# Weight blocks split whole instead of in halves, in a two-layer decoder trunk in split fp32

## The chip, the cores and the metric

The kernel runs on one core of one Trainium2 chip. The metric is the device time of one execution in microseconds (us), the median of several runs.

## The reference

A token matrix `x` (256 tokens, 2048 wide) goes through two layers, each a token mixer followed by a SwiGLU. A vector `c` gives a shift, a scale and a gate for every sub-layer.

```python
for i in range(2):
    sh1, sc1, g1, sh2, sc2, g2 = split(silu(c) @ w_mod[i] + b_mod[i], 6)
    h = rms_norm(x, norm1_g[i]) * (1 + sc1) + sh1
    y = retention_mixer(h, ...) if i == 0 else short_conv_mixer(h, ...)   # 8 heads / width 3
    x = x + g1 * y
    h = rms_norm(x, norm2_g[i]) * (1 + sc2) + sh2
    a, b = split(h @ ffn_w_in[i], 2)                  # 2048 -> 2 x 5632
    x = x + g2 * ((silu(a) * b) @ ffn_w_out[i])       # 5632 -> 2048
return rms_norm(x, final_g)
```

All of it is in float32, and all weights are read once.

## The kernel before

**Split products.** TensorE multiplies in a type with a shorter mantissa (`float32r`). Every float32 operand is therefore split in two: `hi`, the operand cast to the short type, and `lo`, what is left (`lo = raw - hi`). A product is then three matmuls: hi by hi, hi by lo, lo by hi. The tokens' side is split when it is made. The weights are split as they stream in.

**The weight stream.** All layer weights lie in `w_all` as 456 blocks of 128 partitions by 2048 columns (1 MB each), in the order of use. `fetch` (L370) starts the load of the next block into one of three buffers `raw`. `prepare` (L376) takes the next *piece* of a block: ScalarE casts it (`nc.scalar.copy(hi, raw)`, L402), then VectorE subtracts (`lo = raw - hi`, L405). In the kernel before a piece is half a block, 1024 columns; `hi` and `lo` have four buffers of 1024 columns each (`PART_BUFS`). `take` (L410) hands the matmuls their columns. Each time a piece is used up, `take` calls `prepare` until the piece in use and two more are ready (`AHEAD`; three more in the last stage, `ahead_now`). A cast has to wait until the matmuls on the buffer's old content are done. VectorE and ScalarE each work through their queue in order; the order was set by a scheduler when the program was built, except in the opening, where it is the order of the code. TensorE's order is the order of the code throughout.

**The modulation.** `modulation` (L313) needs one 1 MB block of `w_mod` for each 128 entries of a shift, scale or gate: the load takes one of the same three `raw` buffers, and VectorE multiplies and sums it in one instruction (L318). 32 of them stand in the opening (L755), 160 are spread over the kernel by `paced`.

**The stages.** The opening computes the first norm and the first weights' products beside the modulation, with both engines' order written by hand. Then come the retention's heads and its output product, the SwiGLU of layer 0, the short convolution, and the SwiGLU of layer 1, the *last stage*.

**The last stage and its sevens.** Here the roles are turned round: 128 tokens by 128 rows are the weights of the array, and 512 columns of a weight block are streamed. `gathered` (L1269) goes through the *rows* of one pass: a row is one block, two row tiles by two column tiles of 512. A plain row is 24 matmuls (`by_token`). Three rows of each pass are *sevens* (`Seven`, L155): a Strassen-Winograd product of 2 by 2 parts, seven products (`thrice`) of three matmuls each instead of eight. For that the block's four parts B11, B12, B22, B21 (the four 512 columns of `b`) are turned into

- T1 = B12 - B11 and T3 = B22 - B12, written to `differences` (L391, one VectorE instruction, a buffer that there is once),
- T2 = B22 - T1, written over B12 (L395),
- T4 = B21 - T2, written over B21 after B21 has been split (L397).

Before, the pieces of a seven are four: (B22, B21), (T1, T3), (B11, T2), T4. `uses` (L158) gives the order of the products.

A pass of `last_input` (ten of them) has eight rows, of which rows 3, 4 and 6 are sevens (`IN_SEVEN`), so that 3 and 4 follow each other. Before row 2 of the next pass, `turned` brings the result back to the other layout: eight transposes on TensorE (L1331), copies on ScalarE, two subtractions on VectorE (L1336). In five of the ten passes it also makes the sums of tokens that later sevens need (`tokens_sums_of`, L1143 to L1146, and a `split`). In three passes it does not, and in two passes there is no `turned`: the results of the last pass of each part are turned inside the following `last_output`. `mixed_sums` (L1243 to L1246) and four sums (L1317) close a pass. A pass of `last_output` (four of them) has sevens at positions 2, 4 and 6, so that a plain row follows each seven.

Of the kernel before, what the change touches and what calls it, by code (L numbers as in the profile page):

```python
# [11 lines left out]
F32R = mybir.dt.float32r  # L12
I32 = mybir.dt.int32
AF = mybir.ActivationFunctionType
ALU = mybir.AluOpType
PSUM = bass.MemoryType.PSUM

P = 128
# [7 lines left out]
DV = 512  # L26
# [5 lines left out]
CHUNK = 2048  # L32
HALF = 1024
# [11 lines left out]
AHEAD = 2  # L45
# [2 lines left out]
MOD_PRIO = -300  # L48
STEPS = (8, 8, 20)
RAW_BUFS = 3  # L50
PART_BUFS = 4
LEFT, ENDS, EARLIER = 8, 2, 120

Q0, K0, V0, G0 = 0, HEADS * DK, 2 * HEADS * DK, 2 * HEADS * DK + HEADS * DV
# [3 lines left out]
class Group:  # L58
# [11 lines left out]
    def uses(self):  # L70
        return [(self, k, c, w) for k in self.ks for c, w in self.items]
# [70 lines left out]
class Seven:  # L142
# [6 lines left out]
    n = 2 * DV // P  # L149
# [6 lines left out]
        return [(i, a, DV), (i, b, DV), (j, b, DV), (j, a, DV)]  # L156

    def uses(self):  # L158
        return [(self, None, n, DV) for n in ("B22", "B21", "T1", "T3", "B11", "T2", "T4")]


def in_pairs(cols, rows, sevens):
# [94 lines left out]
def trunk(ctx: ExitStack, tc: tile.TileContext, x_in, c_in, pos_in, w_mod, cols_in, gain_in, tab_in, w_all, out):  # L257
    nc = tc.nc
    const = ctx.enter_context(tc.tile_pool(name="const", bufs=1))
    work = ctx.enter_context(tc.tile_pool(name="work", bufs=2))  # L260
    wpool = ctx.enter_context(tc.tile_pool(name="wpool", bufs=PART_BUFS))
    ps = ctx.enter_context(tc.tile_pool(name="ps", bufs=8, space=PSUM))
# [3 lines left out]
    def name(s):  # L266
        serial[0] += 1
        return f"{s}_{serial[0]}"

    def tmp(tag, shape=(P, S), dtype=F32, pool=work, bufs=None):  # L270
        return pool.tile(list(shape), dtype, tag=tag, name=name(tag), bufs=bufs)
# [9 lines left out]
    x = [t[:, j, :] for t in x4 for j in range(4)]  # L281
    n_cols = cols_in.shape[1]
    cols = const.tile([P, n_cols], F32, tag="cols", name="cols")
    at = [0]
# [16 lines left out]
    differences = flat[2]  # L301
# [35 lines left out]
    early = sum(g.n * len(g.ks) for g in RET_SPANS)  # L337
# [15 lines left out]
    def needed(layer, which, last=KT - 1):  # L353
        while any(m[:2] == (layer, which) and m[2] <= last for m in todo):
            modulation(*todo.pop())
# [6 lines left out]
    in_seven, n = set(), 0  # L362
# [2 lines left out]
            in_seven.add(n // CHUNK)  # L365
        n += g.n * P * len(g.ks)

    pieces = [(i, p) for i in range(w_all.shape[0]) for p in ((2, 3, 4, 5) if i in in_seven else (0, 1))]

    def fetch():  # L370
        raw = wpool.tile([P, CHUNK], F32, tag="raw", name=name("raw"), bufs=RAW_BUFS)
# [4 lines left out]
    def prepare(between=None):  # L376
        if prepared[0] == len(pieces):
            return
        _, piece = pieces[prepared[0]]
        prepared[0] += 1  # L380
        if piece in (0, 2):
            if not fetched:
                fetch()
            raws[:] = [fetched.pop(0)]
            while first <= units[0] < early and len(fetched) < RAW_BUFS - 1 and n_fetched[0] < w_all.shape[0]:
                fetch()
        whole = raws[0]
        b = [whole[:, i : i + DV] for i in range(0, CHUNK, DV)]
        raw = whole[:, :HALF] if piece in (0, 4) else whole[:, HALF:]
        if piece == 2:  # L390
            nc.vector.tensor_tensor(differences, whole[:, DV : 3 * DV], whole[:, : 2 * DV], op=ALU.subtract)  # L391
        elif piece == 3:
            raw = differences
        elif piece == 4:
            nc.vector.tensor_tensor(b[1], b[2], differences[:, :DV], op=ALU.subtract)  # L395
        elif piece == 5:
            nc.vector.tensor_tensor(b[3], b[3], b[1], op=ALU.subtract)  # L397
            raw = b[3]
        width = raw.shape[1]
        hi = wpool.tile([P, HALF], F32R, tag="hi", name=name("hi"))[:, :width]  # L400
        lo = wpool.tile([P, HALF], F32R, tag="lo", name=name("lo"))[:, :width]
        nc.scalar.copy(hi, raw)  # L402
        if between:
            between()
        nc.vector.tensor_tensor(lo, raw, hi.bitcast(F32), op=ALU.subtract)  # L405
        ready.append((hi, lo, width))

    prepared, ahead_now = [0], [AHEAD]

    def take(group, k, col, width=P):  # L410
# [89 lines left out]
        return banks  # L500

    def summed(pt, dst=None, at=slice(0, S)):
        low = tmp("low", bufs=3)
        nc.scalar.copy(low[:, at], pt[:, 1, at])
        dst = tmp("sum", bufs=4) if dst is None else dst
        nc.vector.tensor_tensor(dst, pt[:, 0, at], low[:, at], op=ALU.add)
        return dst
# [96 lines left out]
    def normed(accs, layer, norm, g):  # L604

        needed(layer, SH2 if norm else SH1)  # L610
        shift = mod_s[layer][norm].unsqueeze(2)
        ends = [raw_all[:, :, i : i + 1] for i in range(ENDS)]
        nc.scalar.copy(ends[0], shift)
        nc.vector.tensor_tensor(ends[1], shift, ends[0].bitcast(F32), op=ALU.subtract)
        banks = [bank().rearrange("p a b -> p (a b)")[:, : S + 2] for _ in g.cols]
        made = [0]

        def more(n):
            while made[0] < n:
                modulated(h[made[0]], made[0], root, layer, norm)  # L620
                made[0] += 1

        for k in g.ks:
            high, low = raw_all[:, k, : ENDS + S], raw_all[:, k, ENDS + S :]
            for c, pt in zip(g.cols, banks):
                hi, lo = take(g, k, c)
                nc.tensor.matmul(pt, hi, high, start=k == 0, stop=False, skip_group_check=True)  # L627
                nc.tensor.matmul(pt[:, 2:], hi, low, start=False, stop=False, skip_group_check=True)  # L628
                nc.tensor.matmul(pt, lo, high, start=False, stop=k == KT - 1, skip_group_check=True)  # L629
            if k == ROOTS_AT:  # L630
                r = norm_roots(norm_sums(accs), D)
            elif k == SPREAD_AT:
                root = tmp("rb", bufs=1)
                nc.scalar.copy(root, norm_spread(r))
            elif k > SPREAD_AT:
                more(min(k, made[0] + 2))
        more(KT)
        paced(len(g.cols) * len(g.ks))

        def total(pt, dst=None):  # L640
            low_end = tmp("end", (P, 1), bufs=4)
            nc.scalar.copy(low_end, pt[:, 1:2])
            end = tmp("end", (P, 1), bufs=4)
            nc.scalar.activation(end, pt[:, 0:1], AF.Identity, bias=low_end)
            t = tmp("low", bufs=3)
            nc.vector.tensor_tensor(t, pt[:, 2:], root, op=ALU.mult)
            dst = tmp("sum", bufs=4) if dst is None else dst
            nc.scalar.activation(dst, t, AF.Identity, bias=end)
            return dst

        return [lambda dst=None, pt=pt: total(pt, dst) for pt in banks]
# [27 lines left out]
    with ExitStack() as inner:  # L679
# [64 lines left out]
        with tc.tile_pool(name="start", bufs=1) as sp:  # L744
# [133 lines left out]
            at = 0.0  # L878
# [205 lines left out]
    for i, g in enumerate(CONV_IN):  # L1084
        pending += [sums(g)] if i else normed(acc, 1, 0, g)
        while len(pending) >= 3:
# [3 lines left out]
            b, c, u = pb(tmp("bsum", pool=mpool, bufs=2)), pc(), pu()  # L1090
# [67 lines left out]
    def made_in_sums():  # L1158

        tmp("beside_sums", (P, BESIDE_SUMS), bufs=1)  # L1160
        for tag, n in (("u", 3), ("low", 3), ("sum", 4)):
            single_sums.extend(tmp(tag, (P, 2, P), F32R, bufs=n) for _ in range(n))
        for i in IN_SEVEN:
            both = tmp("u512", (P, 2, S), pool=mpool, bufs=3)
            for n in range(2):
                k = 2 * i + n
                high, low = [h[k].bitcast(F32)[:, v, :] for v in range(2)]
                nc.vector.tensor_tensor(both[:, n, :], high, low, op=ALU.add)
            in_sums[i] = [single_sums.pop() for _ in range(3)]
            tokens_sums_of(*parts(both), h[2 * i][:, :, P:], in_sums[i])  # L1170
# [53 lines left out]
    def sevens(g, act, base, sums, ours, banks, first, last):  # L1224

        s1, s2, s4 = [[v[:, n, :] for n in range(2)] for v in sums]
        (a11, s3), (a12, a22) = [[half_of(act[k - base], t) for t in range(2)] for k in g.ks]
        p1, p5, p6, p7 = [(b, first, last) for b in banks]
        for use, x, (o, a, z) in zip(g.uses(), (s4, a12, s1, s3, a11, s2, a22), (
            (ours[0, 1], False, False), (ours[0, 0], False, False), p5, p7, p1, p6, (ours[1, 0], False, False)  # L1230
        )):
            thrice(o, x, take(*use), a, z)
            if use[2] in ("B21", "T3", "T2"):
                paced(4)
        paced(4)

# [151 lines left out]
    for part in range(2):  # L1388
        n = LAST_TILES[part] // 2
        mid = mids(LAST_TILES[part]) if part else first_mid  # L1390
        if not part:
            first_rows(mid[-2:])
            made_in_sums()
            ahead_now[0] = AHEAD + 1
        for i, groups in enumerate(LAST_IN[part]):
            due = OUT_SEVEN[part]
            seven = [tokens_sums[due.index(q)] if q in due else None for q in (2 * i, 2 * i + 1)]
            last_input(groups, mid[2 * i : 2 * i + 2], seven)
        act = [mid[k // 2][:, k % 2] for k in range(2 * n)]
        for c, groups in enumerate(LAST_OUT[part]):  # L1400
            last_output(part, 2 * c, groups, act, part * LAST_TILES[0])
# [37 lines left out]
```

## Time and profile before

| | us |
|---|---|
| median of 3 runs | 2593.82 |
| lowest and highest run | 2591.88, 2595.02 |
| span of the profiled execution | 2591.5 |
| TensorE busy | 2563.3 |
| VectorE busy | 2197.4 |
| ScalarE busy | 1306.0 |

The span runs from the first to the last instruction of one profiled execution; no device time of that execution itself is given, and the runs lie 0.4 to 3.5 us above its span. The profile names engines PE (TensorE), PEld (its weight load), DVE (VectorE), ACT (ScalarE), POOL (GpSimd) and SP (the queue of the loads). A group of instructions is shown as line, engine, operation, output<-input, shape and count, then busy time, mean ns of one, and the idle time of the engine just before them with what ended it.

### The profile page before, as it was taken

To read this page: it belongs to the slowest core of one execution; us is meant where nothing else is said; L and a number is where in the kernel's file an instruction comes from. 1 tells how busy PE (TensorE), PEld (TensorE's weight loads), DVE (VectorE), ACT (ScalarE), POOL (GpSimd) and SP (SyncE) were. 2 spreads that over 40 slices of the span, in tenths; PEclk is the share of its full clock that TensorE was granted. 3 is DMA by queue.
4 is the path that set the end of the run, shared out by engine and by line. 5 is a ranking of instruction groups with operands and counts; after the bars stand their busy time and mean duration, and the time that the engine had idled before them with its cause. 6 is when DMAs were issued, how large, how long until landed. Compare 5 with 4: busy or idle time off the path is not lost.

```text
span 2591.5 us, 36408 instructions
## 1 busy us (share of the span) xinstructions
PE 2563.3 (99%) x14181; PEld 2236.3 (86%) x14181; DVE 2197.4 (85%) x2762; ACT 1306.0 (50%) x1792; POOL 125.9 (5%) x232
## 2 busy tenths in 40 slices
PE   7999999999999999999999999999999999999998
PEld 6898889888889888888888898888998888888887
DVE  7988978787698887777778889988989998999978
ACT  5544543444456545334444454444565554556554
POOL 0000000110000000100001001000000000000001
PEclk9999999999999999999999999999999999999999
DMA  9975768767676888777877768877845565555654
GB/s 398 388 293 209 268 243 306 300 248 277 251 282 246 330 323 307 301 296 298 298 294 283 298 237 313 330 297 277 308 165 210 188 223 205 180 210 187 222 208 147
DMA packets 96688, 689.56 MB, mean 266 GB/s; under 512 B 10737, under 2 KB 12161, under 8 KB 13441
## 3 DMA queue, kind: packets, MB, share of 16 engines
q1 hardware_dynamic: 96514, 687.23, 71.3%
q8 instruction: 111, 1.82, 0.3%
q14 instruction: 63, 0.52, 0.1%
HBM read 685.08 MB, written 2.11 MB: 265 GB/s over the span
## 4 chain that ended last, share of the span: by engine, by line
PE 94%; DVE 3%; DMA 2%; issue 1%; ACT 1%; ACTq 0%; POOLq 0%; POOL 0%; DVEq 0%
PE bank L447 30%; PE bank L450 16%; PE bank L461 12%; PE bank L460 12%; PE bank L462 12%; PE bank L495 2%; PE bank L496 2%; PE bank L494 2%; PE bank L627 1%; PE bank L629 1%; PE bank L628 1%; DVE raw L755 1%; DMA raw<-w_all 1%; DVE lo L405 1%; PE bank L983 1%
## 5 line engine op out<-in xcount | busy, mean ns | idle before, releaser
L402 ACT CAST hi<-raw 128x1024 fp32r<-128x1024 f32 (+1 forms) x954 | 978.9, 1033 | 1015.8 <-PE bank L447 346.4
L405 DVE TENSOR_TENSOR lo<-raw,hi 128x1024 fp32r<-128x1024 f32 (+1 forms) x954 | 1133.9, 1197 | 322.6 <-ACT hi L402 317.3
L447 PE MATMUL bank<-h,hi 128*128 128x512 f32 x2016 | 699.3, 390 | 0.0
L450 PE MATMUL bank<-h,lo 128*128 128x256 f32 x2016 | 568.5, 282 | 0.0
L447 PEld LDWEIGHTS bank<-h,hi 128*128 128x128 f32 x2016 | 378.4, 188 | 79.2
L460 PE MATMUL bank<-hi,h 128*128 128x512 f32 x1032 | 405.0, 392 | 2.2 <-DVE rm L739 2.2
L461 PE MATMUL bank<-lo,h 128*128 128x512 f32 x1032 | 404.3, 392 | 0.0
L462 PE MATMUL bank<-hi,h 128*128 128x512 f32 x1032 | 402.7, 390 | 0.0
L450 PEld LDWEIGHTS bank<-h,lo 128*128 128x128 f32 x2016 | 381.0, 189 | 0.1
L318 DVE SCALAR_TENSOR_TENSOR raw<-raw,cb 128x2048 f32<-128x2048 f32 x160 | 365.5, 2284 | 15.7 <-DMA raw<-w_mod 15.3
L447 PE MATMUL bank<-mid,hi 128*128 128x512 f32 x922 | 319.8, 390 | 0.0
L450 PE MATMUL bank<-mid,lo 128*128 128x256 f32 x922 | 260.1, 282 | 0.4 <-DVE lo L405 0.4
L460 PEld LDWEIGHTS bank<-hi,h 128*128 128x128 f32 x1032 | 194.4, 188 | 40.7 <-DVE rm L739 2.8
L462 PEld LDWEIGHTS bank<-hi,h 128*128 128x128 f32 x1032 | 194.2, 188 | 40.8
L461 PEld LDWEIGHTS bank<-lo,h 128*128 128x128 f32 x1032 | 194.5, 188 | 40.4 <-DVE lo L405 3.3
L447 PEld LDWEIGHTS bank<-mid,hi 128*128 128x128 f32 x922 | 173.1, 188 | 36.2
L450 PEld LDWEIGHTS bank<-mid,lo 128*128 128x128 f32 x922 | 174.2, 189 | 0.7 <-DVE lo L405 0.7
L447 PE MATMUL bank<-rm,hi 128*128 128x512 f32 x496 | 172.5, 390 | 0.0
L496 PE MATMUL bank<-h,lo 128*128 128x256 f32 x512 | 146.4, 286 | 4.6 <-DVE lo L405 4.6
L494 PE MATMUL bank<-h,hi 128*128 128x256 f32 x512 | 146.1, 285 | 3.4 <-ACT h L783 3.4
L495 PE MATMUL bank<-h,hi 128*128 128x256 f32 x512 | 146.1, 285 | 0.7 <-DVE h L784 0.7
L450 PE MATMUL bank<-rm,lo 128*128 128x256 f32 x496 | 139.8, 282 | 0.0
(256 smaller groups left out, 3197.4 us busy)
## 6 DMA issues: line engine op xcount, KB each, us to landing
raw<-w_all SPq DMA_DIRECT2D x456, 1024.0 KB, 4.8
raw<-w_mod SPq DMA_DIRECT2D x192, 1024.0 KB, 5.2
x<-x_in SPq DMA_DIRECT2D x4, 512.0 KB, 5.3
out<-xt SPq DMA_DIRECT2D x4, 512.0 KB, 3.0
decay<-tab_in SPq DMA_DIRECT2D x8, 128.0 KB, 2.4
x<-gate_row SPq DMA_DIRECT2D x2, 512.0 KB, 4.8
last_gain<-gain_in SPq DMA_DIRECT2D x1, 1024.0 KB, 7.2
cols<-cols_in SPq DMA_DIRECT2D x1, 152.0 KB, 8.3
```

The source lines that it names most:

```text
L318: nc.vector.scalar_tensor_tensor(raw, raw, 1.0, cb, op0=ALU.mult, op1=ALU.mult, accum_out=total)
L402: nc.scalar.copy(hi, raw)
L405: nc.vector.tensor_tensor(lo, raw, hi.bitcast(F32), op=ALU.subtract)
L447: nc.tensor.matmul(pt, hi, h, start=fresh and k == g.ks[0], stop=False, skip_group_check=True)
L450: nc.tensor.matmul(pt[:, 1, :], lo, h[:, 0, :], start=False, stop=last and k == g.ks[-1], skip_group_check=True)
L460: nc.tensor.matmul(o, hi, w_hi, start=first, stop=False)
L461: nc.tensor.matmul(o, hi, w_lo, start=False, stop=False)
L462: nc.tensor.matmul(o, lo, w_hi, start=False, stop=last)
L494: nc.tensor.matmul(pt, hi, h[:, 0, :], start=first, stop=False, skip_group_check=True)
L495: nc.tensor.matmul(pt, hi, h[:, 1, :], start=False, stop=False, skip_group_check=True)
L496: nc.tensor.matmul(pt, lo, h[:, 0, :], start=False, stop=last, skip_group_check=True)
L627: nc.tensor.matmul(pt, hi, high, start=k == 0, stop=False, skip_group_check=True)
```

## The change

Behind the opening a plain block is one piece: one cast and one subtraction of 2048 columns (piece 5). The blocks of the opening stay in halves (pieces 0 and 1), but both halves go into one buffer. `hi` and `lo` have three buffers of 2048 columns instead of four of 1024. A seven has three pieces: the whole block with T2 already in the place of B12 (piece 2), the differences (piece 3), and T4 (piece 4); the last two share a buffer. The order of a seven's products is changed to fit: B11, T2, B22, B21, T1, T3, T4. `ahead_now` stays at two pieces in the last stage. The room for the larger buffers comes from one buffer `low` less and from the reserved space of the descriptor ring, which goes from its default to 512.

```diff
-PART_BUFS = 4
+PART_BUFS = 3
...
-        return [(self, None, n, DV) for n in ("B22", "B21", "T1", "T3", "B11", "T2", "T4")]
+        return [(self, None, n, DV) for n in ("B11", "T2", "B22", "B21", "T1", "T3", "T4")]
...
-    pieces = [(i, p) for i in range(w_all.shape[0]) for p in ((2, 3, 4, 5) if i in in_seven else (0, 1))]
+    halved = early * P // CHUNK
+    pieces = [
+        (i, p) for i in range(w_all.shape[0])
+        for p in ((2, 3, 4) if i in in_seven else (0, 1) if i < halved else (5,))
+    ]
...
-        if piece in (0, 2):
+        if piece in (0, 2, 5):
...
-        raw = whole[:, :HALF] if piece in (0, 4) else whole[:, HALF:]
-        if piece == 2:
+        raw, at = whole, 0
+        if piece in (0, 1):
+            raw = whole[:, piece * HALF : (piece + 1) * HALF]
+            at = piece * HALF
+        elif piece == 2:
             nc.vector.tensor_tensor(differences, whole[:, DV : 3 * DV], whole[:, : 2 * DV], op=ALU.subtract)
+            nc.vector.tensor_tensor(b[1], b[2], differences[:, :DV], op=ALU.subtract)
         elif piece == 3:
             raw = differences
         elif piece == 4:
-            nc.vector.tensor_tensor(b[1], b[2], differences[:, :DV], op=ALU.subtract)
-        elif piece == 5:
             nc.vector.tensor_tensor(b[3], b[3], b[1], op=ALU.subtract)
-            raw = b[3]
+            raw, at = b[3], HALF
         width = raw.shape[1]
-        hi = wpool.tile([P, HALF], F32R, tag="hi", name=name("hi"))[:, :width]
-        lo = wpool.tile([P, HALF], F32R, tag="lo", name=name("lo"))[:, :width]
+        if at == 0:
+            both[:] = [wpool.tile([P, CHUNK], F32R, tag=tag, name=name(tag)) for tag in ("hi", "lo")]
+        hi, lo = [t[:, at : at + width] for t in both]
         nc.scalar.copy(hi, raw)
...
-        low = tmp("low", bufs=3)
+        low = tmp("low", bufs=2)
...
-        for use, x, (o, a, z) in zip(g.uses(), (s4, a12, s1, s3, a11, s2, a22), (
-            (ours[0, 1], False, False), (ours[0, 0], False, False), p5, p7, p1, p6, (ours[1, 0], False, False)
+        for use, x, (o, a, z) in zip(g.uses(), (a11, s2, s4, a12, s1, s3, a22), (
+            p1, p6, (ours[0, 1], False, False), (ours[0, 0], False, False), p5, p7, (ours[1, 0], False, False)
...
-            if use[2] in ("B21", "T3", "T2"):
+            if use[2] in ("T2", "B21", "T3"):
...
-            ahead_now[0] = AHEAD + 1
...
-    nc = bacc.Bacc("TRN2", target_bir_lowering=False, num_devices=1)
+    nc = bacc.Bacc("TRN2", target_bir_lowering=False, num_devices=1, dynamic_dma_scratch_size=512)
```

More of the change, by code (lines that the diff above doesn't have):

```diff
@@ L406, in prepare @@
         ready.append((hi, lo, width))
+    both = []
     prepared, ahead_now = [0], [AHEAD]
@@ L644, in total @@
             nc.scalar.activation(end, pt[:, 0:1], AF.Identity, bias=low_end)
-            t = tmp("low", bufs=3)
+            t = tmp("low", bufs=2)
             nc.vector.tensor_tensor(t, pt[:, 2:], root, op=ALU.mult)
@@ L1160, in made_in_sums @@
         tmp("beside_sums", (P, BESIDE_SUMS), bufs=1)
-        for tag, n in (("u", 3), ("low", 3), ("sum", 4)):
+        for tag, n in (("u", 3), ("low", 2), ("sum", 4)):
             single_sums.extend(tmp(tag, (P, 2, P), F32R, bufs=n) for _ in range(n))
```

## The prediction

> **What bounds the kernel now.** I read the page's shares first, then the stages, then one pass of the last stage.
>
> ```profile
> span 2591.5 us, 36408 instructions
> ...
> PE 2563.3 (99%) x14181; PEld 2236.3 (86%) x14181; DVE 2197.4 (85%) x2762; ACT 1306.0 (50%) x1792; POOL 125.9 (5%) x232
> ...
> PE 94%; DVE 3%; DMA 2%; issue 1%; ACT 1%; ACTq 0%; POOLq 0%; POOL 0%; DVEq 0%
> ```
>
> TensorE is busy 99% of the span and holds 94% of the chain that ended last. What it does not use is 28 us. The table by stage (us, then busy us of PE, PEld, DVE, ACT) tells where that is:
>
> ```profile
> 0.00:128.00 128.00, 110.67 (x625) 93.37 (x625) 110.56 (x121) 71.97 (x112) 1.57 (x5) 1.00 0.98 397
> 128.00:810.00 682.00, 681.03 (x3951) 603.45 (x3952) 561.61 (x722) 321.64 (x444) 42.78 (x74) 1.00 0.71 266
> 810.00:1530.00 720.00, 720.00 (x4234) 641.47 (x4233) 578.38 (x695) 342.00 (x489) 53.70 (x104) 1.00 0.80 299
> 1530.00:1890.00 360.00, 359.57 (x2190) 323.40 (x2189) 320.52 (x457) 175.16 (x257) 19.84 (x41) 1.00 0.79 292
> ...
> 1935.00:2105.00 170.00, 170.00 (x762) 139.87 (x762) 157.36 (x185) 98.23 (x114) 0.00 (x0) 1.00 0.58 204
> 2105.00:2210.00 105.00, 104.46 (x463) 86.23 (x462) 90.20 (x105) 54.03 (x59) 0.00 (x0) 1.00 0.56 202
> 2210.00:2460.00 250.00, 250.00 (x1118) 205.81 (x1117) 231.69 (x274) 145.06 (x167) 0.00 (x0) 1.00 0.56 201
> ```
>
> 17.3 us of it lie in the opening. From 128 to 2460 us TensorE is idle for 1.9 us in all. So the body has nothing to win, and the question is where this change makes TensorE wait. In the last stage (from 1935 us) VectorE is 93% busy: 157.36 of 170, 231.69 of 250. There it has no room.
>
> **One pass of the last stage now.** Between two turns of the result (eight transposes, from the chain) lies one pass of eight rows:
>
> ```profile
> 2019.30 0.87 PE bank L1331 x8
> ...
> 2061.91 0.87 PE bank L1331 x8
> ```
>
> That is 42.61 us. Its matmuls follow at this distance:
>
> ```profile
> 2000.10 0.39 PE L460 MATMUL bank<-hi,h 128*128 128x512 f32 x1
> 2000.32 0.39 PE L461 MATMUL bank<-lo,h 128*128 128x512 f32 x1
> 2000.55 0.39 PE L462 MATMUL bank<-hi,h 128*128 128x512 f32 x1
> 2000.78 0.39 PE L460 MATMUL bank<-hi,h 128*128 128x512 f32 x1
> ```
>
> 0.68 us for three, 0.227 each. A plain row (24) takes 5.44 us, a seven (21) 4.76; five, three and the turn make 42.35. TensorE loses 0.25 us in a pass. VectorE in the same pass:
>
> ```profile
> L405 DVE TENSOR_TENSOR lo<-raw,hi 128x1024 fp32r<-128x1024 f32 x16 | 19.4, 1220 | 2.4 <-ACT hi L402 2.2
> L405 DVE TENSOR_TENSOR lo<-x,hi 128x1024 fp32r<-128x1024 f32 x3 | 3.7, 1221 | 0.2 <-ACT hi L402 0.2
> ```
>
> It idles 2.6 us of 42.6, for casts. Any new idle time beyond that and it is VectorE that sets the pass.
>
> **What the wider instructions cost.** ScalarE first, then VectorE, over the whole span:
>
> ```profile
> L402 ACT CAST hi<-raw 128x1024 fp32r<-128x1024 f32 x912 | 953.9, 1052 | 980.2 <-PE bank L447 346.4 <-PE bank L462 305.6 <-DMA raw<-w_all 179.9
> ...
> L402 ACT CAST hi<-raw 128x512 fp32r<-128x512 f32 x42 | 26.1, 620 | 35.6 <-PE bank L462 32.3 <-DVE lo L405 3.3
> ```
>
> ```profile
> L405 DVE TENSOR_TENSOR lo<-raw,hi 128x1024 fp32r<-128x1024 f32 x912 | 1107.2, 1221 | 315.9 <-ACT hi L402 310.8
> ...
> L405 DVE TENSOR_TENSOR lo<-raw,hi 128x512 fp32r<-128x512 f32 x42 | 28.8, 686 | 6.7 <-ACT hi L402 6.5
> ```
>
> From 512 to 1024 columns the cast grows by 432 ns and the subtraction by 535. Twice that on top gives 1.92 us for a whole cast and 2.29 for a whole subtraction, estimates by a straight line. Two halves take 2.10 and 2.44: each whole block saves 0.18 us on ScalarE and 0.15 on VectorE. In a queue without waits the distance of two subtractions is shorter than their length, as this stretch of VectorE shows:
>
> ```profile
> 2021.60 0.68 DVE L1336 TENSOR_TENSOR mid<-bank,mid 128x512 fp32r<-128x512 f32 x1
> 2022.20 0.28 DVE L1143 TENSOR_TENSOR u<-u 128x128 f32<-128x128 f32 x1
> ...
> 2023.81 1.21 DVE L391 TENSOR_TENSOR x<-raw 128x1024 f32<-128x1024 f32 x1
> 2024.95 0.55 DVE L512 TENSOR_TENSOR in_cb<-u,in_cb 128x384 fp32r<-128x384 f32 x1
> 2025.42 1.81 DVE L405 TENSOR_TENSOR lo<-raw,hi 128x1024 fp32r<-128x1024 f32 x2
> 2027.15 0.68 DVE L395 TENSOR_TENSOR raw<-raw,x 128x512 f32<-128x512 f32 x1
> 2028.13 1.23 DVE L405 TENSOR_TENSOR lo<-raw,hi 128x1024 fp32r<-128x1024 f32 x1 [0.30 <-ACT hi L402]
> ```
>
> 0.60 us for 512 columns, 1.14 for 1024, so 2.22 for 2048.
>
> **Part 1: plain blocks behind the opening, nothing.** Before, a cast waits for the buffer four pieces back and can begin three halves ahead of its use, 8.2 us; cast and subtraction of a half (2.27) leave a lead of 5.9 (a half of a plain row is 2.72 us). After, three whole buffers let it begin two blocks ahead, 10.9 us; 4.21 leave 6.7. `raw` is given back earlier too: before, when its second half is subtracted, 8.2 - 2.7 - 2.3 = 3.2 us ahead of the block's use; after, 6.7 ahead. So the loads in SP's queue (the modulation's among them, which the built order puts one weight load later) run no closer to their need. An instruction on VectorE that comes due just behind a subtraction waits up to 1.1 us longer (2.29 - 1.22), one on ScalarE 0.9. Sums into PSUM's eight banks hide that; in the three norms and the ends of the output products it could show: 0 to 2 us at each of four, 0 to 8. The other bound is the 1.9 us of idle above, all won. I take 0, the row of 810 to 1530 us (720.00 of 720 busy) being nearest. The buffer `low` and the ring cost nothing: no queue of GpSimd's own moves data here. In the opening each engine's order is unchanged, the blocks stay in halves.
>
> **Part 2: the sevens, the term that counts.** A seven's first piece is now the whole block with T2 in it. Its cast can't begin before the differences and T2 are done on VectorE; its subtraction can't begin before the cast is done. Before, the first piece (B22, B21) needed neither, and other pieces' subtractions filled the casts (the stretch above: T2 at 2027.15, then only 0.30 of waiting). In the changed program's built order VectorE's queue around rows 3 and 4, both sevens, is: subtraction of row 2; row 3's differences, T2, whole subtraction; the turn's work; row 3's differences' subtraction, T4; row 4's differences; row 3's T4 subtraction; row 4's T2; row 4's whole subtraction. So behind each T2 VectorE stands idle for a cast of 1.92 us.
>
> I follow it with 0 where TensorE begins row 3. The last pass ended at -17.2 (turn and three rows). VectorE then has three closing sums (1.8), row 1's subtraction (2.22), one sum and two products (1.8), row 2's subtraction (2.22): -9.0. Differences and T2 (1.14 + 0.60): -7.2. Cast: -5.3. Whole subtraction: -3.0. The turn's work with the sums of tokens (2021.60 to 2025.42 above, less 1.14): 2.68, -0.3. Then 1.14 + 0.60 + 1.14 + 0.60 + 0.60 up to row 4's T2: 3.8. Cast 5.7, subtraction 8.0. TensorE wants row 4's hi at 4.76 and its lo at 4.99: it waits **3.0 us**. Then T4's subtractions: row 4's stands behind row 5's whole one (8.0 + 1.14 + 0.60 + 2.22 + 0.60 = 12.6; wanted after 18 matmuls and one more, 4.3 us behind the row's begin at 7.8, so at 12.1): 0.5. Row 6's stands behind row 7's, whose cast has to wait for row 5's buffer, free when row 6 begins and the last matmul has drained (0.39 long at a distance of 0.23, so 0.2 later): 0.2 + 1.92 + 2.29 + 0.60 = 5.0 into row 6, wanted at 4.3: 0.7. In sum 4.2 us.
>
> In a pass whose turn makes no sums of tokens the turn's work is 1.2 instead of 2.68: 1.5 + 0.5 + 0.7 = 2.7. Without a turn 0.3 + 0.5 + 0.7 = 1.5. Five, three and two such passes: 21.0 + 8.1 + 3.0 = 32.1. In the four output passes a plain row follows each seven, and sums and T4 fill VectorE's casts; but the row behind the first seven takes the buffer of the row before it, free when the seven begins, and VectorE's queue reaches its subtraction late: from the last pass's end (two plain rows ahead, -10.7) four closing sums, differences, T2 and five gate operations (4 x 0.60 + 1.14 + 6 x 0.60) to -3.6, the whole subtraction to -1.3, six operations (2 x 1.14 + 4 x 0.60) to 3.4, row 3's subtraction to 5.6, wanted at 4.99: 0.6 each, 2.4. Two of them hold a turn besides, at 1.2 and 2.7 by the same rows: 3.9. Sum 38.4. The 0.25 us a pass lost now falls under it: 2.5 off. **+36 us.**
>
> The whole of VectorE's pass says the same: 40.0 busy now (42.6 - 2.6), less 0.15 for each of five plain rows, plus three casts of idle (5.8) and 1.5 of waiting for the pass to end: 46.5 against 42.35.
>
> The Trainium skill speaks against this change: "Perfetto Trace Analysis", section Optimizing Scalar/DVE Operations, has larger operations help a saturated engine, but says that where these engines cause bubbles elsewhere, breaking instructions up may let work be completed sooner. By its first half the last stage would gain under 1 us a pass; the rows give the second half the greater weight.
>
> **Rivals.** *The clock falls too.* After two waits in the opening the granted clock (the column behind POOL) fell:
>
> ```profile
> 120.00:125.00 5.00, 5.00 (x35) 4.57 (x33) 5.00 (x7) 2.10 (x2) 0.00 (x0) 1.00 1.01 421
> 125.00:130.00 5.00, 2.83 (x10) 1.84 (x9) 5.00 (x6) 0.00 (x0) 0.00 (x0) 0.81 0.51 192
> 130.00:135.00 5.00, 5.00 (x32) 4.74 (x31) 4.05 (x7) 3.66 (x6) 0.00 (x0) 0.84 1.01 418
> ```
>
> TensorE idled 2.2 us in 125 to 130 and then lost 19% and 16% of the clock over ten us, 1.75 us. If 3 us of waiting does the same in eight passes, that is 8 x 1.75 = 14: 2593.8 + 36 + 14 = 2644. Against it: VectorE, not TensorE, would then set the pass, and hides part. "TensorE: Matmul & The Clock Gate", section The HAM clock gate, of the Trainium skill has the clock halved after an idle window of about 3.4 us; by that rule our waits would mostly stay under it, while the rows above show a fall after less.
>
> *The wait is hidden, so that the change does nothing to the time.* If casts begin earlier than I have them, or VectorE catches up in rows 5 to 7, only T4's waits and the outputs' stay, or less: 2590 to 2602. For it: VectorE's load falls, and 2.6 us of idle are there. Against: the order is fixed, and T2, cast and subtraction are a chain of 4.8 us in it wherever it starts.
>
> *Faster.* The opening's casts wait for buffers:
>
> ```profile
> ACT hi L402 <- PE bank L462: 57.9, 38, 5.2
> ```
>
> ```profile
> 50.00:75.00 25.00, 23.67 (x145) 20.81 (x146) 23.43 (x24) 15.86 (x25) 0.00 (x0) 1.00 1.01 420
> 75.00:100.00 25.00, 24.21 (x157) 21.90 (x156) 23.96 (x25) 15.70 (x23) 0.00 (x0) 1.00 0.98 387
> 100.00:128.00 28.00, 26.21 (x165) 23.24 (x163) 26.32 (x30) 12.61 (x17) 0.00 (x0) 1.00 0.96 396
> ```
>
> That is 57.9 us of ScalarE in the first 230. Now six halves instead of four fit. If these waits hold TensorE up, VectorE's 4.3 us of idle time from 50 to 128 us go, and the 2.5 in the passes: 2593.8 - 6.8 = 2587. It decides only if the sevens cost under 2 us. That VectorE is 94% busy there, in an unchanged order, and the loads' engines 96 to 101%, speaks against it.
>
> **How the numbers follow.** The span is 2591.5, the median 2593.8; the runs lie up to 3.5 above the span, and I add to the median: 2593.8 + 36 = **2630 us**. Forecast (2602 to 2638) 0.64, the clock too (to 2660) 0.17, hidden 0.12, faster 0.07. The low end, 2602, is a quarter of the sevens' cost; the high end, 2660, has the clock, the 8 us of part 1 and some more for the turns. About 0.2% (5 us) is what a measurement can tell here: faster 0.07, same 0.09, slower 0.84.
>
> **What would show it.** Right: TensorE idle in the last stage, in waits of L460 and L461 for casts and subtractions (L409, L412), 4 us in passes with sums of tokens, the distance of turns 46 to 47 us; 128 to 1890 us as now within a few us; VectorE's idle time in front of whole subtractions of sevens. Wrong: turns still 42.6 apart, or time lost before 1890 us, or loads that come late.

## The result and the profile after

The changed kernel takes **2634.28 us** (median of 4 runs, 2633.03 to 2635.51); the kernel before, on the same chip, takes 2592.85 (4 runs, 2591.82 to 2595.02). The ratio is 1.016, with a 95% interval of 1.0147 to 1.0174: slower by 41 us. The profiled execution of the changed kernel spans 2633.7 us, 42.2 more than that of before.

The page of the kernel after, its shares and its chain:

```profile
span 2633.7 us, 35071 instructions
...
PE 2577.2 (98%) x14181; PEld 2237.0 (85%) x14181; DVE 2159.9 (82%) x2336; ACT 1233.2 (47%) x1366; POOL 170.8 (6%) x232
...
PE 82%; DVE 10%; ACT 3%; issue 2%; DMA 2%; ACTq 0%; POOLq 0%; POOL 0%; DVEq 0%; SPq 0%
```

VectorE is busy for 38 us less and ScalarE for 73 us less, in 426 and 426 fewer instructions; so the wider instructions do save time. Yet VectorE and ScalarE now hold 10% and 3% of the chain, where they held 3% and 1%. The table by stage of the kernel after (us, then busy us of PE, PEld, DVE, ACT and POOL, and the granted clock) says where:

```profile
0.00:128.00 128.00, 109.96 (x625) 92.98 (x625) 109.93 (x120) 72.87 (x114) 1.58 (x5) 1.00 0.97 397
128.00:810.00 682.00, 677.20 (x3926) 598.99 (x3926) 549.88 (x615) 304.90 (x336) 45.80 (x74) 1.00 0.72 267
810.00:1530.00 720.00, 720.00 (x4233) 641.56 (x4232) 569.85 (x565) 319.22 (x359) 91.19 (x104) 1.00 0.80 298
...
1935.00:2105.00 170.00, 161.95 (x705) 130.01 (x704) 141.29 (x140) 86.00 (x78) 0.00 (x0) 0.99 0.45 172
...
2210.00:2460.00 250.00, 239.50 (x1036) 193.62 (x1035) 207.30 (x209) 120.22 (x106) 0.00 (x0) 0.98 0.48 183
2460.00:2634.00 174.00, 161.13 (x708) 130.53 (x706) 137.55 (x134) 79.94 (x75) 14.98 (x8) 0.98 0.46 176
```

Up to 1530 us only the second row has changed. In the last stage TensorE, which was busy 170.00 of 170 and 250.00 of 250, now misses 8.05 and 10.5 us, its clock there is 0.99 and 0.98 (the 0.98 of the last row belongs to the end of the program, where the clock is halved from 2628.71 us on), and VectorE, once 93% busy there, is at 83%: both idle, so they wait for each other. TensorE's order is the same in both kernels, so its matmuls can be matched one by one. The matched starts lie apart by +0.6 us at the end of the opening; by -0.8 at 200 us, because the profiled execution of before spends 3.41 us at half the clock from 128.15 us on and this one does not; and by +0.6 again at 700 us. (Of this rise of 1.4 us 0.6 lie at 231 us, where TensorE waits for `sp`, which VectorE makes behind a whole subtraction; the rest lies near 525 and 633 us.) Then come +2.5 around the norm at 780 us, -0.7 at 1813 us, and **+40.0 in the last stage**, 42.3 in all.

What TensorE waits for in the last stage (1935 us to the end, the view of waits; total, times, longest):

```profile
PE bank L469 <- DVE lo L412: 24.2, 30, 1.8
PE bank L468 <- ACT hi L409: 0.2, 1, 0.2
```

Nearly all of it is `lo`, the result of the subtraction. (This view counts idle time only from the modelled end of the matmul before; by the distance of starts the waits are longer, 2.09 us where it has 1.82.) The turns of the result, three that follow each other:

```profile
2025.84 1.03 PE L1339 MATMUL bank<-tab,x 128*128 128x128 f32 x8
...
2071.96 1.03 PE L1339 MATMUL bank<-tab,x 128*128 128x128 f32 x8
...
2119.36 1.03 PE L1339 MATMUL bank<-tab,x 128*128 128x128 f32 x8
```

46.12 and 47.40 us, where it was 42.61 and 42.72 (the third turn stands in an output pass). Now the inside of the pass that begins at 2025.84, on VectorE (start, duration, in brackets the idle time before and what ended it):

```profile
2021.88 1.22 DVE L398 TENSOR_TENSOR x<-raw 128x1024 f32<-128x1024 f32 x1
2023.13 0.69 DVE L399 TENSOR_TENSOR raw<-raw,x 128x512 f32<-128x512 f32 x1
2025.93 2.29 DVE L412 TENSOR_TENSOR lo<-raw,hi 128x2048 fp32r<-128x2048 f32 x1 [2.11 <-ACT hi L409]
...
2034.31 0.68 DVE L399 TENSOR_TENSOR raw<-raw,x 128x512 f32<-128x512 f32 x1
2037.00 2.29 DVE L412 TENSOR_TENSOR lo<-raw,hi 128x2048 fp32r<-128x2048 f32 x1 [2.02 <-ACT hi L409]
...
2047.80 2.29 DVE L412 TENSOR_TENSOR lo<-raw,hi 128x2048 fp32r<-128x2048 f32 x1 [2.10 <-ACT hi L409]
```

on ScalarE:

```profile
2035.06 1.91 ACT L409 CAST hi<-raw 128x2048 fp32r<-128x2048 f32 x1 [1.76 <-PE bank L470]
```

and on TensorE:

```profile
2037.03 0.50 PE L468 MATMUL bank<-hi,h 128*128 128x512 f32 x1
2039.35 0.50 PE L469 MATMUL bank<-lo,h 128*128 128x512 f32 x1 [1.82 <-DVE lo L412]
...
2043.89 0.50 PE L469 MATMUL bank<-lo,h 128*128 128x512 f32 x1 [0.19 <-DVE lo L412]
...
2055.05 0.50 PE L469 MATMUL bank<-lo,h 128*128 128x512 f32 x1 [0.53 <-DVE lo L412]
```

These four views are one story. At 2034.31 VectorE makes T2 of row 4. Just behind it (2035.06) ScalarE can begin the whole cast. VectorE has nothing else ahead of the whole subtraction in its queue, idles 2.02 us and starts it at 2037.00. TensorE began row 4 at 2037.03, did the first matmul on `hi`, and had to wait for `lo` until 2039.35. The three bracketed idle times on VectorE are the three sevens of the pass, about 2 us each.

The bracket of the cast names a matmul, the one whose signal came last by the profile. That the cast waits for T2 can be seen in the same row of a later pass, where the bracket names T2's line; in both the cast begins 0.08 us behind the end of T2:

```profile
2374.32 1.91 ACT L409 CAST hi<-raw 128x2048 fp32r<-128x2048 f32 x1 [1.76 <-DVE raw L399]
```

After such waits the granted clock (the third number from the right) can fall. In this trace it is 1.00 or 0.50 and changes only on a grid of 3.41 us: its falls in the last stage begin at 2085.99, 2331.75, 2379.54 and 2427.32 us, which is 72, 14 and 14 steps apart, and each lasts one step. Steps of this grid, two around row 4's wait of the pass above and three around that of the next pass:

```profile
2034.80:2038.21 3.41, 2.73 (x12) 1.75 (x10) 1.39 (x2) 3.15 (x3) 0.00 (x0) 1.00 0.71 283
2038.21:2041.63 3.42, 2.28 (x10) 1.93 (x11) 3.42 (x4) 2.06 (x2) 0.00 (x0) 1.00 0.06 24
2082.58:2085.99 3.41, 1.59 (x6) 0.84 (x5) 2.86 (x2) 3.26 (x3) 0.00 (x0) 1.00 0.55 228
2085.99:2089.41 3.42, 3.42 (x9) 2.66 (x9) 3.42 (x4) 0.62 (x1) 0.00 (x0) 0.50 0.00 0
2089.41:2092.82 3.41, 3.41 (x16) 2.79 (x15) 2.38 (x3) 0.83 (x1) 0.00 (x0) 1.00 0.66 221
```

The wait is the same, but in the first pass it is split between two steps, which leave TensorE idle for 0.68 and 1.14 us, and in the second it lies in one, with 1.82 us of idle time; the step behind that one has half the clock. That is why the second distance of turns is longer.

The 2.5 us at 780 us lie at a norm, where the next product needs `h`. VectorE after, then TensorE after, then VectorE before:

```profile
777.02 2.29 DVE L318 SCALAR_TENSOR_TENSOR raw<-raw,cb 128x2048 f32<-128x2048 f32 x1
...
779.86 2.29 DVE L412 TENSOR_TENSOR lo<-raw,hi 128x2048 fp32r<-128x2048 f32 x1 [0.15 <-ACT hi L409]
...
783.20 0.18 DVE L622 TENSOR_TENSOR h<-s,h 128x16 fp32r<-128x16 f32 x1
```

```profile
783.52 0.36 PE L635 MATMUL bank<-h,hi 128*128 128x258 f32 x1 [2.45 <-DVE h L622]
```

```profile
780.12 0.18 DVE L614 TENSOR_TENSOR h<-s,h 128x16 fp32r<-128x16 f32 x1
780.22 2.28 DVE L318 SCALAR_TENSOR_TENSOR raw<-raw,cb 128x2048 f32<-128x2048 f32 x1
```

In both kernels one step of the modulation (L318) stands right behind the norm's last operation and one ahead of it. Before, the one ahead ran at 774.12 us, 6.0 us earlier than that operation, with only halves behind it; after, it runs at 777.02, a whole subtraction follows, and TensorE waits. How much of the 2.5 us each of the two makes was not separated.

### The profile page after: what moved, and what is told of

It reads as the page before. It is cut to its first block, busy times and chain, and to the rows that moved or that the text cites. A ratio compares the mean times of both kernels' runs of the same rounds, so it can differ in the third digit from the quotient of the medians.

```text
span 2633.7 us, 35071 instructions
## 1 busy us (share of the span) xinstructions
PE 2577.2 (98%) x14181; PEld 2237.0 (85%) x14181; DVE 2159.9 (82%) x2336; ACT 1233.2 (47%) x1366; POOL 170.8 (6%) x232
## 3 DMA queue, kind: packets, MB, share of 16 engines
q8 instruction: 111, 1.82, 0.3%
## 4 chain that ended last, share of the span: by engine, by line
PE 82%; DVE 10%; ACT 3%; issue 2%; DMA 2%; ACTq 0%; POOLq 0%; POOL 0%; DVEq 0%; SPq 0%
PE bank L455 29%; PE bank L458 16%; PE bank L469 9%; PE bank L470 9%; PE bank L468 8%; DVE lo L412 6%; ACT hi L409 3%; PE bank L504 2%; PE bank L503 2%; PE bank L502 2%; DMA raw<-w_all 2%; PE bank L635 1%; PE bank L637 1%; PE bank L636 1%; DVE raw L763 1%
## 5 line engine op out<-in xcount | busy, mean ns | idle before, releaser
L412 DVE TENSOR_TENSOR lo<-raw,hi 128x2048 fp32r<-128x2048 f32 (+2 forms) x528 | 1073.2, 2039 | 340.5 <-ACT hi L409 339.2
L409 ACT CAST hi<-raw 128x2048 fp32r<-128x2048 f32 (+2 forms) x528 | 898.8, 1710 | 941.3 <-PE bank L455 296.2
L318 DVE SCALAR_TENSOR_TENSOR raw<-raw,cb 128x2048 f32<-128x2048 f32 x160 | 365.7, 2286 | 67.0 <-DMA raw<-w_mod 66.9
```

Source lines behind the costliest of these rows:

```text
L318: nc.vector.scalar_tensor_tensor(raw, raw, 1.0, cb, op0=ALU.mult, op1=ALU.mult, accum_out=total)
```

## The experiments

The theory from the prediction, called the chain theory: the order differences, T2, whole cast, whole subtraction is one chain of 4.8 us in VectorE's queue, and two sevens that follow each other leave it too little time. Rivals: the buffers (three places, of which a seven takes two, so that casts start late) and the load (queues that are simply longer). All edits are against the changed kernel, and the order of VectorE's and ScalarE's queues is built anew for each.

**The sevens back in four pieces, whole plain blocks kept.**

```diff
-        return [(self, None, n, DV) for n in ("B11", "T2", "B22", "B21", "T1", "T3", "T4")]
+        return [(self, None, n, DV) for n in ("B22", "B21", "T1", "T3", "B11", "T2", "T4")]
...
-        for p in ((2, 3, 4) if i in in_seven else (0, 1) if i < halved else (5,))
+        for p in ((2, 3, 6, 4) if i in in_seven else (0, 1) if i < halved else (5,))
...
-            nc.vector.tensor_tensor(b[1], b[2], differences[:, :DV], op=ALU.subtract)
+            raw = whole[:, HALF:]
         elif piece == 3:
-            raw = differences
+            raw, at = differences, HALF
+        elif piece == 6:
+            nc.vector.tensor_tensor(b[1], b[2], differences[:, :DV], op=ALU.subtract)
+            raw = whole[:, :HALF]
...
```

> Plain blocks stay whole as in the change, three whole buffers too, but a seven goes back to its four pieces and its old order of products: (B22, B21), (T1, T3), (B11, T2), T4. Chain theory (differences, T2, whole cast, whole subtraction in a row): the last stage's turns come back to 42.6 to 43.5 us apart, no granted clock under 0.95 there, and the time is the kernel before plus the 3 us lost near 780 us: 2594 to 2602. Buffer theory (three whole buffers let casts begin too late): turns stay at 45 to 47, over 2620. Load theory (VectorE has too much work in a pass): a seven in four pieces has more instructions, so 2634 or more.

Measured: 2596.97 us, ratio 1.0015 (1.0005 to 1.0024). The last stage is healed: two turns of it, from the chain,

```profile
2020.75 0.87 PE bank L1342 x8
2063.14 0.87 PE bank L1342 x8
```

are 42.39 us apart, 0.04 above the floor of 42.35 and 0.22 under before. This kernel has more instructions than the changed one and the same three buffers, so neither the load nor the buffers by themselves make the loss. What is left of the loss lies elsewhere: at the norm,

```profile
781.62 0.36 PE L638 MATMUL bank<-h,hi 128*128 128x258 f32 x1 [2.51 <-DVE h L625]
```

with 3.41 us of half the clock behind this wait, 4.0 us together by matched starts, and in the output passes (149.08 us between the turns of the two parts, 148.18 before).

**The plain blocks back in halves, the sevens in three pieces.**

```diff
-    halved = early * P // CHUNK
+    halved = w_all.shape[0]
```

> All plain blocks go back to two halves (sharing a whole buffer), the sevens stay in three pieces as in the change. Chain theory: turns as in the change (44.7 and 47.3), the loss near 780 us gone: 2628 to 2634. If whole plain blocks were the cause of the last stage's loss: turns back under 44 and the time under 2605.

Measured: 2624.01 us, 1.0118 (1.0103 to 1.0133), 4 us under the expected. TensorE's waits in the last stage are the same kind (and 1.7 us on `hi`):

```profile
PE bank L469 <- DVE lo L412: 18.7, 19, 1.8
```

The wait at the norm is gone (30.00 of 30 us busy from 770 to 800), so that one is the whole plain blocks' doing. The last stage costs 32.3 us instead of 40.0. So the sevens' pieces alone make 32, and whole plain blocks add 7.7 where the sevens already are late, though alone (the run before this one) they add nothing in the input passes. Where those 7.7 come from in detail was not separated.

**T2 made behind the whole cast.** The decisive one: the same number of instructions, of the same widths, in the same buffers; the differences and T2 are only written later, T2 next to T4, so that the whole cast no longer depends on them. The product with T2 then multiplies B12 in its place, so this part of the result differs.

```diff
-        elif piece == 2:
+        elif piece == 3:
             nc.vector.tensor_tensor(differences, whole[:, DV : 3 * DV], whole[:, : 2 * DV], op=ALU.subtract)
-            nc.vector.tensor_tensor(b[1], b[2], differences[:, :DV], op=ALU.subtract)
-        elif piece == 3:
             raw = differences
         elif piece == 4:
+            nc.vector.tensor_tensor(b[1], b[2], differences[:, :DV], op=ALU.subtract)
             nc.vector.tensor_tensor(b[3], b[3], b[1], op=ALU.subtract)
```

> The change with two instructions moved: a seven's whole block is cast before the differences and T2 are made (the product with T2 therefore uses B12 instead, so that part of the result is another one), and T2 is made ahead of T4. The same instructions, sizes and buffers. Chain theory: the waits of 2.1 us go, the row behind a seven still gets its buffer late (up to 0.5 us each), T4's 0.8 us may stay: turns 42.7 to 44.2, time 2597 to 2610. Buffer theory and load theory: nothing changes, 2630 to 2636.

Measured: 2611.23 us, 1.0068 (1.0053 to 1.0083), just above the expected range. The turns come after 43.67 us,

```profile
2024.39 0.87 PE bank L1338 x8
2068.06 0.87 PE bank L1338 x8
```

and the waits of row 4 are gone; the last stage costs 15.2 us by matched starts instead of 40.0. So 23 of the 41 us hung on this one dependence, the fall of the clock behind its waits among them. Buffers and load, which are unchanged here, would have left the time at 2630 or above. What remains is one wait in row 5, the plain row behind the two sevens:

```profile
2041.47 0.50 PE L468 MATMUL bank<-lo,h 128*128 128x512 f32 x1 [0.99 <-DVE lo L411]
```

```profile
2037.39 1.22 DVE L398 TENSOR_TENSOR x<-raw 128x1024 f32<-128x1024 f32 x1
2038.53 5.09 DVE L411 TENSOR_TENSOR lo<-raw,hi 128x512 fp32r<-128x512 f32 x3
```

Its subtraction is the second of the three in the last line: it begins 0.60 us behind 2038.53 and lasts 2.29, to 2041.42, and from 2032.72 on VectorE has hardly idled. So this remainder looks like a matter of load; no run shows it apart.

**No sums of tokens.** The turns leave out the sums that later sevens need; their places hold zeros.

```diff
-                if of is not None:
-                    tokens_sums_of(*parts(both), dst[:, 0, :, P:], of)
```

> The change without the sums of tokens inside the turn (four small VectorE operations and two splits; the sums used later are zeros). Chain theory: those 1.5 us of VectorE stand in the chain of row 4's T2, so the five passes with them fall from 47.1 to the 44.7 of the others, and the clock no longer falls: 2634 less 12, less up to 3 in the first output pass: 2618 to 2624. Load theory: the same order of saving, 1.5 us in each of six, 9 us: 2625. Buffer theory: 2632 to 2635.

Measured: 2624.20 us, 1.0119 (1.0104 to 1.0134), just above the expected 2618 to 2624 and next to the 2625 of the load theory, so the time alone does not tell these two apart. The turns do: all their distances over input passes lie between 44.68 and 44.73 us (44.85 from the last of them into an output pass), as in the turn-only passes of the changed kernel (44.71). No wait on `lo` in the last stage is longer than 1.3 us, and the clock does not fall there before the end of the program (mean over the execution 0.998 instead of 0.996). So the turn's work on VectorE is the part of row 4's wait that differs between the kinds of passes, as the prediction had it.

**Where whole plain blocks pay.** Two kernels with the sevens in four pieces: halves up to the block 136 (past the norm), and halves up to the block 332 (whole blocks only in the last stage).

```diff
-    halved = early * P // CHUNK
+    halved = 136
...
+    halved = 332
```

> The sevens in four pieces of the first experiment, and plain blocks in halves up to block 136 (behind the first norm of a SwiGLU, near 780 us), whole from there on. If the 2.7 us wait there comes from a whole subtraction in front of the norm's last operations: it goes, the last stage keeps its 42.4 us between turns, and the time is the kernel before less 0.2 for each of ten passes: 2589 to 2594 beside 2593.3. If the wait has another cause (the order of the modulation's loads), 2595 to 2598 as in the first experiment.

> As the one before, but whole blocks begin only in the last stage (block 332). Turns 42.4 us apart, everything ahead of 1890 us as in the kernel before: 2589 to 2594. If whole blocks win something between 800 and 1890 us, this one is slower than the one before by that; TensorE shows no idle time there, so no difference over 1 us is expected.

Measured: 2592.11 us (0.9999, 0.9991 to 1.0008) and 2591.92 us (1.0000, 0.9991 to 1.0009). The 196 blocks between them make no difference that can be measured, though each whole block saves ScalarE 0.18 and VectorE 0.15 us: nobody waits for that time.

**T2 behind, and the plain blocks in halves as well.** This was to take away the wait of row 5.

```diff
-    halved = early * P // CHUNK
+    halved = w_all.shape[0]
```

> Sevens in three pieces with T2 made behind the whole cast (the product with T2 uses B12 instead, so that part of the result is another one), and all plain blocks in halves. The 1.0 us that a pass still lost with T2 behind stood in front of row 5, whose whole cast waits for a buffer until row 4 begins. With halves the second half's subtraction is off that path: turns 42.4 to 43.0, 2592 to 2600. If the rest has to do with the seven's own whole subtraction, turns stay at 43.7: 2606 to 2610.

Measured: 2645.73 us, 1.0205 (1.0191 to 1.0219), a miss for each theory: the slowest kernel of all, with turns 48.1 us apart. Its rows on VectorE and on TensorE:

```profile
2043.64 0.69 DVE L402 TENSOR_TENSOR raw<-raw 128x512 f32<-128x512 f32 x1
...
2046.51 2.89 DVE L411 TENSOR_TENSOR lo<-raw,hi 128x2048 fp32r<-128x2048 f32 x2
```

```profile
2046.56 0.50 PE L467 MATMUL bank<-hi,h 128*128 128x512 f32 x1 [1.15 <-ACT hi L408]
2049.45 0.51 PE L468 MATMUL bank<-lo,h 128*128 128x512 f32 x1 [2.39 <-DVE lo L411]
```

TensorE waits for T4 of row 4. VectorE had made T4 (L402) by 2044.33, but its split stands second in both queues, behind row 6's whole cast and whole subtraction: the row x2 at 2046.51 is 2048 columns first and the 512 of T4 behind them. In the run with T2 behind and whole plain blocks the 512 stood first. So a change of the plain blocks alone, through the order that was built from it, put a whole block of a row that is needed later ahead of a small piece that is needed now: 3.5 us per pass and a fall of the clock (0.99 on average). Whether the remainder of the run with T2 behind is load stays open.

**The best parts together.** The runs so far say: leave the sevens in four pieces, and use whole blocks only where VectorE has no idle time to lose. First the ten input passes alone. Both edits come on top of the sevens in four pieces.

```diff
+        for p in ((2, 3, 6, 4) if i in in_seven else (5,) if 332 <= i < 364 or 384 <= i < 432 else (0, 1))
```

> Sevens in four pieces in the old order; whole plain blocks only in the ten input passes of the last stage (blocks 332 to 363 and 384 to 431), halves everywhere else, the output passes included. Chain theory: the input passes keep the 0.22 us each won by the kernel with whole blocks in the whole last stage (turns 42.39 apart instead of 42.61, 2.2 us in ten passes), the four output passes no longer lose 0.8 to 1.1 us each: 2589.5 to 2592, ratio 0.999 to 1.000, at the edge of what can be measured. Rival (saved time on ScalarE and VectorE comes through wherever whole blocks stand): less gain than with whole blocks in the whole stage, 2592 or more.

Measured: 2586.94 us against 2593.56, ratio **0.9978 (0.9968 to 0.9988)**: faster than before, and by more than expected. Turns are 42.39 apart as forecast, but the output passes, in halves now, not only stop losing: 147.19 us lie between the turns of the parts, 148.18 before. They hold no whole blocks. So the last kernel takes the whole blocks out everywhere. Of the change it keeps the larger `hi` and `lo`, and what came with them: one buffer `low` less, the smaller space for the ring, and two pieces ahead instead of three in the last stage.

```diff
+        for p in ((2, 3, 6, 4) if i in in_seven else (0, 1))
```

> Sevens in four pieces in the old order and halves everywhere: of the change only the three places of 2048 columns are left, in which six halves find room instead of four. Buffer theory: it is the room that won 0.22 us per input pass, 1.0 in the first two output passes and 0.7 near 1880 us; turns 42.4 apart, 147.2 between the parts' turns, 2586 to 2589 us. Rival, width theory (the whole blocks in the input passes win their 0.22 us each): turns at 42.6, about 2589 to 2591 us.

Measured: 2587.57 us against 2592.00, ratio **0.9982 (0.9973 to 0.9991)**, the same as with whole blocks in the input passes, within the intervals. The turns:

```profile
2017.89 1.03 PE L1342 MATMUL bank<-tab,x 128*128 128x128 f32 x8
```

and the next 42.39 us later, at 2060.28; 147.14 between the parts. In the last stage matched starts gain 3.2 us in both kernels, and 0.7 at 1813 us. So the width of the instructions wins nothing that can be measured. Turns and time came out as the buffer theory said, and room for six halves instead of four is the likely cause; the `low` buffer, the ring and `ahead_now` were not varied alone. Two of the waits that this kernel removes stand in the list of waits of the kernel before and are missing in this one:

```profile
PE bank L461 <- DVE lo L405: 0.5, 1, 0.5
...
PE bank L450 <- DVE lo L405: 0.4, 1, 0.4
```

## Why the prediction was right, step by step

**The forecast**: 2630 with +36 us, measured 2634 with +41. The mechanism is shown: taking the one dependence away (T2 behind the cast) takes away 23 us with the same instructions, widths and buffers, and taking the sums of tokens away takes the difference between the kinds of passes.

**The durations** were estimated by a straight line at 1.92 and 2.29 us. The groups of the kernel after:

```profile
L412 DVE TENSOR_TENSOR lo<-raw,hi 128x2048 fp32r<-128x2048 f32 x426 | 974.7, 2288 | 324.5 <-ACT hi L409 323.2
L409 ACT CAST hi<-raw 128x2048 fp32r<-128x2048 f32 x426 | 814.4, 1912 | 870.7 <-PE bank L455 296.2 <-PE bank L470 206.4 <-DMA raw<-w_all 131.8
```

**The terms of the last stage.** Measured are differences of matched starts; from each predicted term the 0.25 us per pass that the kernel before already lost is taken off:

| | predicted | measured |
|---|---|---|
| five passes with sums of tokens | 19.8 | 22.5 |
| three passes with the turn only | 7.4 | 6.3 |
| first pass without a turn | 1.3 | 2.3 |
| second one, and four output passes | 7.6 | 8.9 |
| sum | 36 | 40.0 |

The sum is near because errors cancel, and that is luck: the clock, a term that the forecast did not have, makes up for a wait that it had too long. **Row 4's wait**, the largest term, was too large: 3.0 predicted, 2.09 measured (2039.35 less 2037.03, less the usual 0.23). The error lies in the first step of that chain. Row 3 began at 2032.18, and VectorE reached row 3's differences at 2021.88, 10.3 us ahead of it; the prediction, by adding up closing sums and two subtractions, had 9.0 (its own terms add up to 9.2). From T2 to the end of the wait it had 4.2 us (1.92 + 2.29); the rows give 4.4. The wait for T4 was predicted at 0.5 us in row 4 and 0.7 in row 6; by starts, less the usual 0.23, they are 0.35 and 0.68.

**The rival on the clock** was given 0.17 as an addition of 14 us, and came true in part. Four of the five passes with sums of tokens show a fall; they lost 4.67, 4.68, 4.95 and 4.69 us, the one without it 3.52, so beside that one pass the clock cost 4.9 us, a term that the forecast had at nothing. In "TensorE: Matmul & The Clock Gate", section The HAM clock gate, the Trainium skill has the clock halved after an idle window of about 3.4 us, and says that the window runs freely, whatever the kernel does. The trace agrees with the free window, by the grid of 3.41 us above. It does not bear out that a whole window must be idle: 1.82 of 3.41 us was enough. So the rival's condition was not a length of wait alone but where the wait lies on the grid.

**Part 1, nothing for the plain blocks**, was wrong within its bounds of 0 to 8: a norm lost 2.5 us, by the mechanism named there (an instruction due behind a wider subtraction), but with a later step of the modulation ahead of it as well, so more than the 1.1 us given for it. Another 1.4 us were lost between 200 and 700 us, at places that Part 1 did not name; with the plain blocks in halves it was 0.5. In the last stage whole plain blocks cost 7.7 us more beside the sevens. This the prediction did not see apart, as it worked the pass out with them in it.

**The rival "hidden"** falls by the waits shown. **The rival "faster"** had a true core in the wrong place: the kernel with room for six halves gains about 4 us (0.9982), not in the opening but in the last stage and at 1813 us, and the sevens' chain covered it ten times over. "Perfetto Trace Analysis", section Optimizing Scalar/DVE Operations, of the Trainium skill was weighed rightly: VectorE and ScalarE were saved 38 and 73 us, and it is the breaking up, not the grouping, that the runs favour. The section says so of engines that are not saturated, a condition that the prediction left out; VectorE was busy for 93% of the last stage before and 83% after.

**The marks**: turns 46 to 47 us apart in passes with sums (46.1 to 47.6), VectorE idle ahead of whole subtractions of sevens (2.0 to 2.1 each), 810 to 1530 us unchanged: all there. Waits of the first matmul for casts, which the prediction named beside those for `lo`, are all but absent (0.2 us).

## What to carry to other kernels

Before two instructions on an in-order engine are joined, look at which inputs the joined one waits for that the first of the two did not: here joining saved 0.15 us of VectorE per block and put a 1.9 us cast into its queue with nothing beside it, three times per pass. Busy time saved on an engine that nobody waits for is worth nothing (196 whole blocks, no difference), while room to run ahead may be worth something by itself (0.9982 here); so try the larger buffer without the wider instruction. Where a scheduler sets an in-order queue, a new size of piece is also a new order, and must be read again from the trace.

## What the runs showed of the hardware

The granted clock of TensorE moves on a grid of its own. In the traces of all eleven kernels, from TensorE's first full clock on, it is 1.00 or 0.50 and changes only after whole steps of 3.41 us. It fell 41 times, each time behind a step in which TensorE had been idle for 1.76 us or more; behind the other 8233 steps at full clock, with 1.69 us of idle time at most, it did not fall (idle time by the modelled ends of the matmuls). So here the border lies near half a step. A wait of 2.1 us cost a step at half the clock in four passes of the changed kernel, where it lay within one step, and nothing in the fifth, where the grid cut it in two. With waits on `lo` of at most 1.3 us (the kernel without sums of tokens) the clock stayed at 1.00 through the last stage, up to the end of the program.
